# A streaming-encoder layer on one core: the first rows read in another order, the second half's rows two groups sooner

## The chip, the cores and the metric

The kernel runs on one core of a Trainium2 chip. A core has a tensor engine for matmuls (TensorE, PE in the profile), three engines for elementwise work (VectorE or DVE, ScalarE or ACT, GpSimd or POOL), and SyncE (SP), which here issues reads. All of them work through their own instructions in order and wait for each other by semaphores. Sixteen DMA engines move data between the main memory (HBM) and the two on-chip memories, SBUF and PSUM. The metric is the device time of one execution in microseconds; lower is better. Before the change it is 1509.12 us, the median of three runs (1508.5 to 1511.66).

## The reference

One layer of a hybrid encoder is computed for 2048 prompt tokens and 32 sample tokens, in float32. The model dimension is 1024.

```python
h = rmsnorm(x, ln_g)
(q, k, v, gate_a, b_gate, c_gate, u_in, gate_c, merge_a, merge_c) = jnp.split(h @ w_in, split_idx, axis=-1)
q = rope(rmsnorm(q.reshape(b, t, 8, 64), q_norm_g), pos)
k = rope(rmsnorm(k.reshape(b, t, 2, 64), k_norm_g), pos)
attn, new_k, new_v = attend(q, k, v, sink)         # chunks of 64, each sees itself and two before
u = c_gate * u_in
conv = causal convolution of u over 3 tokens       # with conv_past ahead of it
y_a = (attn * silu(gate_a)) @ w_attn_out
y_c = (b_gate * conv * silu(gate_c)) @ w_conv_out
r = x + (sigmoid(merge_a) * y_a + sigmoid(merge_c) * y_c) @ w_o
out = r + sigmoid(r @ w_ple_gate) * (p @ w_ple_proj)
```

`rmsnorm` divides by the root of the mean of squares over the 1024 columns of a token. The lines are cut from the reference; the one on the convolution is put in words.

## The kernel before

**Numbers and products.** Each float32 operand is split into a high part (a cast to `fp32r`, made on ACT) and a low part (the operand less its high part, made on DVE). A product is three matmuls: high by high, high by low, low by high. So each weight tile costs one cast and one subtraction ahead of its matmuls: `w<-wr` on ACT (L231 or L160), then on DVE (L232 or L160). For the projections a scheme of seven products instead of eight is used over two halves of the tokens and of the columns (a product is called p1 to p7). It needs sums of weight blocks (`make_sums`, L352 to L368: tiles `a7_0` to `a7_3` and `sc7` are those of group 7; `quad_sums`, L379 to L384: tiles `a11_58_2` and so on) and sums of rows of x. Groups of columns are numbered g = 0 to 20.

**Stages.** The opening, up to about 90 us, computes p @ w_ple_proj (`pp`, the pieces of the weight are `wppr` raw and `wpp0` to `wpp3` split) and the first mean of squares, and begins with the projection of the first half. Rows of x transposed (`b0_0` to `b0_7` for the first 512 tokens, `b1_0` to `b1_7` for the next) are read by `x_row`, squared (`sq`), added up on DVE, and summed over partitions on PE by eight matmuls with a column of ones (`pr`); `stats` makes the power on POOL, a diagonal (`dg`) on DVE, a transpose on PE (`rps`) and a copy on ACT (`rb`). Then the rows are normed. Up to about 440 us the first half of the tokens is projected, group by group. Then comes the second half, whose rows are read again from HBM (`refill`, tiles `xr`). From about 850 us on come the attention, its gates, and the out-projections.

**What sets the order.** In the opening and from the attention on, the order on every engine is written by a planner in the kernel's own Python code (`manual_schedule`): pieces of work are generators with a rank; each has a time at which it may go on, worked out from the assumed durations in `cost` (L104 to L118) and from what each engine and the DMA wire has been given so far. A lower rank goes first. The list `todo_loads` (L1086 to L1094) is the order of the opening's reads on SP; `stats` is started when eight squares are added, after a delay (L959). From L1254 on, the middle follows the order of the code, and the framework puts in the waits.

**The second half's rows.** A generator `X1 = second_half()` (L582) prepares the second half of the tokens while the first is projected. Its steps are: two means (`rms_rows`, each with ten reads `xt1_j_i_e` at L547, ten squares on ACT at L548, a small operation on DVE at L549, a power on POOL, `dg` at L530, `rps1_j` on PE at L532 and `rb` on ACT at L533), four combinations of rows that are stored to HBM (`xc`), and six steps for quarters (`quadrants`). One step is taken at the last product of a group: `prep = [at_step[0, g, 7] for g in range(7, G)]` (L1257), with G = 21. The scratch tiles (`tmp`) of all these come from one pool of 15 buffers, and SP reads into them in the order of the code, together with the weights.

**Attention.** `attention(e, when)` (L1402) works on 128 tokens. It reads `zq` and `zkv` (q, k and v of the tile) and `cs` (cosines and sines, 64 KB), waits for its time, transposes `zq` and `zkv` on PE (`pq`, `pkv`) and multiplies `cs` by the norm's gains on POOL. `next_loads` (L2008) issues further reads and starts weight splits as long as the planned backlog of ACT (`busy["S"]`) is short.

Of the kernel before, what the change touches and what calls it, by code (L numbers as in the profile page):

```python
# [9 lines left out]
AF = mybir.ActivationFunctionType  # L10
# [32 lines left out]
def tile_hybrid_stream_step(ctx: ExitStack, tc: tile.TileContext, x, xT, pT, wu, consts, rope, ckT, cv_dup,  # L43
# [60 lines left out]
    def cost(key, op, kw):  # L104
        if LATE["V"]:
            return cost_queue(key, op, kw)
        if op == "dma_start":
            return 0.9 if kw.get("accum_op") is not None else 0.57 if key == "G" else 0.42
        n = size(kw["out"])
        if key == "T":  # L110
            return max(0.109, 0.00044 * n + 0.0064)
        if key == "S":
            return 0.2 + 0.00082 * n + (0.13 if kw.get("accum_out") is not None else 0.0)
        if key == "G":
            return 2.03 if kw.get("op") == ALU.pow else 0.35 + 0.0021 * n
        if op == "tensor_reduce":
            return 0.08 + 0.0012 * size(kw["in_"])
        return 0.3 if n <= 16 else 0.13 + 0.0011 * n  # L118
# [51 lines left out]
    def free(tag, n=1):  # L170
        live[tag] -= n
        assert live[tag] >= 0, tag
# [758 lines left out]
    def wpp_piece(h):  # L931
        raw = quad(f"wppr{h}")
        eY.dma_start(out=raw, in_=wu[UPP + h // 2, :, 4 * (h % 2):4 * (h % 2) + 4, :])
        yield {"k": 2}
        wpp[h] = pair(f"wpp{h}")
        go(hilo0(wpp[h][0][:, :512], wpp[h][1][:, :512], raw.rearrange("p a b -> p (a b)"), ("wpp", h), lambda: free("wf")), None, None, -3 if h < 2 else -1)

# [5 lines left out]
    def x_row(j, k):  # L943
        v = B[k // 4, j, k % 4] = xrow(f"b{j}_{k}")
        eY.dma_start(out=v[:, :q0], in_=xT[k * P:(k + 1) * P, j * q0:(j + 1) * q0])
        yield {"k": 1, "@": "S"}
        sq = row(f"sq{j}_{k}")[:, :q0]
        eS.activation(out=sq, in_=v[:, :q0], func=AF.Square, scale=1.0 / 32.0)
        yield {}
# [8 lines left out]
        if ready[j] == 8:  # L958
            go(stats(j), now[0] + 1.8, None, j * 2 - 3)  # L959

# [82 lines left out]
    def sums0():  # L1043
# [10 lines left out]
        sums[0] = {7: sc, 5: a21, 6: a11, 3: a12, 4: a22}  # L1054
        for p, i in WS.items():
            eG.dma_start(out=wsum[0][:, i], in_=sums[0][p])
        for i in range(NP, NW):
# [12 lines left out]
    def split0(i):  # L1070
        while i > len(made):
# [16 lines left out]
                  ({}, (0, constants())), ({"wf": 1}, (-2, wpp_piece(2)))]  # L1088
    todo_loads += [({}, (-2, x_row(0, k))) for k in range(3, 8)] + [({"wf": 1}, (-1, wpp_piece(3)))]
    todo_loads += [({"wf": 1}, (0, raw0(i))) for i in range(2)] + [({"tmp": 1}, (0, p_row(1, k))) for k in range(2)]  # L1090
    todo_loads += [({"wf": 1}, (0, raw0(i))) for i in range(2, 5)]
# [164 lines left out]
    conv_at.update({(1, sets[-1], 3 + c % 2, "DE"[c // 2]): lambda c=c: conv_split(2, (c,)) for c in range(4)})  # L1256
    prep = [at_step[0, g, 7] for g in range(7, G)]  # L1257
    for i, todo in enumerate(steps):
# [140 lines left out]
    def attention(e, when):  # L1399
# [13 lines left out]
        cs = sm.tile([P, 2, 64], F32, tag="cs", name=f"cs{b}_{i}")  # L1413
        eY.dma_start(out=cs[:n], in_=rope[cols])
        landed_at = fin[0]
# [8 lines left out]
        for j in range(2):  # L1424
            eT.transpose(out=pkv[:n, j * P:(j + 1) * P], in_=zkv[:, j, :n], identity=ident)
        ab = sm.tile([P, 2, 2, 64], F32, tag="ab", name=f"ab{b}_{i}", bufs=1)
        eG.tensor_tensor(out=ab[:n], in0=cs[:n].unsqueeze(1).to_broadcast([n, 2, 2, 64]),
# [566 lines left out]
    def next_loads():  # L1994
# [36 lines left out]
        while n_split[0] < len(worder) and room["w"] > 0:  # L2031
# [11 lines left out]
            else:  # L2043
                if landed.get(i, 1e9) > now[0] or busy["S"] >= now[0] + (0.3 if i > used[0] + 2 else 1.5):
                    break
# [168 lines left out]
```

## Time and profile before

| what | value |
|---|---|
| median of three runs | 1509.12 us |
| the profiled execution | 1508.07 us |
| its span | 1506.0 us |
| mean granted clock of TensorE | 0.998 |
| data moved | 378.34 MB, 251 GB/s |
| longest single PE wait | 1.5 us |

The span is the time from the first to the last instruction in the profile. Busy times of the engines are shown further below, where they are used. A row of the timeline reads: start, duration, engine, line, operation, tiles written and read, shape, count, and in brackets the idle time before it and what ended it. A row of the windows reads: the stretch and its length, then the busy time and the number of instructions of PE, of the weight loads, of DVE, ACT and POOL, then the granted clock, the busy share of the DMA engines, and GB/s. The DMA engines by stretches of a fortieth of the span (37.65 us), in tenths, and the rate:

```profile
DMA  9469886898777987533578885687988959989959
GB/s 353 154 246 348 314 291 221 276 347 271 253 274 256 340 292 262 186 127 122 153 243 312 288 270 181 210 253 218 302 207 272 240 157 258 312 247 283 256 168 286
```

### The profile page before, as it was taken

The numbers are of one execution on the slowest core, as the hardware profiler recorded it, in microseconds if no ns is written. First come the engines' busy times: TensorE is split into PE (matmuls) and PEld (weight loads), VectorE is DVE, ScalarE is ACT, GpSimd is POOL, SyncE is SP. The second block draws the span as 40 slices with busy tenths as digits, with TensorE's granted clock in tenths as the row PEclk, the third lists the DMA queues.
The fourth block names the chain that finished last, engine by engine and source line by source line (L and its number), as shares of the span: only waits on it lengthen the run. The fifth ranks groups of instructions, "written<-read, shape, count | busy, mean of one in ns | idle before, by whom it ended". The sixth has DMA issues, their size and how long they took to land.

```text
span 1506.0 us, 28005 instructions
## 1 busy us (share of the span) xinstructions
PE 1489.3 (99%) x9553; PEld 1348.6 (90%) x9553; DVE 1210.7 (80%) x2308; ACT 803.7 (53%) x1910; POOL 399.0 (26%) x582
## 2 busy tenths in 40 slices
PE   9999999999999999999999999999999999999998
PEld 7878888888889999999999989998888788999998
DVE  7897887885579788799976878778899999676777
ACT  8453244344457655434455646687765686342453
POOL 2133332332211443433323311113232202211201
PEclk9999999999999999999999999999999999999999
DMA  9469886898777987533578885687988959989959
GB/s 353 154 246 348 314 291 221 276 347 271 253 274 256 340 292 262 186 127 122 153 243 312 288 270 181 210 253 218 302 207 272 240 157 258 312 247 283 256 168 286
DMA packets 206670, 378.34 MB, mean 251 GB/s; under 512 B 24896, under 2 KB 58496, under 8 KB 206528
## 3 DMA queue, kind: packets, MB, share of 16 engines
q1 hardware_dynamic: 160608, 258.30, 52.6%
q0 software_dynamic: 36272, 100.44, 22.2%
q10 hardware_dynamic: 9648, 17.83, 3.2%
q8 instruction: 75, 1.23, 0.3%
q14 instruction: 67, 0.55, 0.1%
HBM read 246.53 MB, written 130.04 MB: 250 GB/s over the span
## 4 chain that ended last, share of the span: by engine, by line
PE 91%; DMA 4%; DVE 2%; ACT 1%; issue 1%; POOL 0%; SPq 0%; DVEq 0%; ACTq 0%; POOLq 0%
PE b L160 21%; PE a L654 8%; PE a L651 7%; PE a L649 7%; PE yB L160 6%; PE yA L160 5%; PE la L787 5%; PE c L651 4%; PE c L649 4%; PE c L654 4%; PE lc L787 2%; PE pp L160 2%; PE O L160 2%; PE S L160 2%; PE PT L160 1%; PE lb L787 1%
## 5 line engine op out<-in xcount | busy, mean ns | idle before, releaser
L160 PE MATMUL b<-xb_h,w 128*128 128x264 f32 (+1 forms) x1344 | 310.7, 322 | 1.4 <-DVE at L160 1.4
L160 PEld LDWEIGHTS b<-xb_h,w 128*128 128x128 f32 x1344 | 222.7, 188 | 19.5 <-DVE at L160 1.9
L651 PE MATMUL a<-x_l,w 128*128 128x264 f32 (+1 forms) x744 | 228.2, 320 | 0.0
L649 PE MATMUL a<-x_h,w 128*128 128x264 f32 (+1 forms) x744 | 227.4, 320 | 0.2 <-ACT w L231 0.2
L160 PE MATMUL b<-xb_l,w 128*128 128x264 f32 (+1 forms) x672 | 216.6, 322 | 0.0
L654 PE MATMUL a<-x_h,w 128*128 128x264 f32 (+1 forms) x744 | 199.7, 321 | 0.9 <-DVE w L232 0.9
L231 ACT CAST w<-wr 128x512 fp32r<-128x512 f32 (+1 forms) x180 | 110.5, 619 | 96.2 <-PE c L654 34.9
L232 DVE TENSOR_TENSOR w<-wr,w 128x512 fp32r<-128x512 f32 (+1 forms) x180 | 133.2, 748 | 29.6 <-ACT w L231 28.0
L649 PEld LDWEIGHTS a<-x_h,w 128*128 128x128 f32 x744 | 139.9, 188 | 11.3 <-ACT w L231 0.4
L651 PEld LDWEIGHTS a<-x_l,w 128*128 128x128 f32 x744 | 140.0, 188 | 10.9
L654 PEld LDWEIGHTS a<-x_h,w 128*128 128x128 f32 x744 | 124.0, 188 | 11.9 <-DVE w L232 1.2
L160 PEld LDWEIGHTS b<-xb_l,w 128*128 128x128 f32 x672 | 126.4, 188 | 8.5
L160 ACT CAST w<-wr 128x512 fp32r<-128x512 f32 x120 | 73.6, 622 | 98.4 <-PE b L160 51.5
L787 PE MATMUL la<-x_h,w 128*128 128x264 f32 x516 | 111.3, 285 | 1.6 <-ACT w L231 1.6
L651 PE MATMUL c<-x_l,w 128*128 128x512 f32 (+1 forms) x336 | 110.9, 340 | 0.0
L649 PE MATMUL c<-x_h,w 128*128 128x512 f32 (+1 forms) x336 | 110.5, 339 | 0.0
L231 ACT CAST w<-a 128x512 fp32r<-128x512 f32 x82 | 49.8, 620 | 98.6 <-DVE a L364 33.2
L654 PE MATMUL c<-x_h,w 128*128 128x512 f32 (+1 forms) x336 | 100.1, 339 | 0.0
L160 DVE TENSOR_TENSOR w<-wr,w 128x512 fp32r<-128x512 f32 x120 | 83.6, 705 | 18.0 <-ACT w L160 17.7
L848 DVE SCALAR_TENSOR_TENSOR u<-u,c 128x264 f32<-128x264 f32 (+1 forms) x125 | 59.5, 507 | 42.8 <-ACT u L843 26.1
L160 PE MATMUL yB<-ycs_h,w 128*128 128x264 f32 (+1 forms) x384 | 91.0, 325 | 0.0
L160 PE MATMUL yA<-ac_h,w 128*128 128x264 f32 (+1 forms) x384 | 90.5, 323 | 0.0
(443 smaller groups left out, 3889.7 us busy)
## 6 DMA issues: line engine op xcount, KB each, us to landing
wr<-in_wu SPq DMA_DIRECT2D x161, 256.0 KB, 4.8
a<-in_wu SPq DMA_DIRECT2D x116, 256.0 KB, 5.3
wr<-ws SPq DMA_DIRECT2D x74, 256.0 KB, 4.0
w<-o SPq DMA_DIRECT2D x32, 512.0 KB, 4.7
ws<-a POOLq DMA_DIRECT2D x63, 256.0 KB, 4.3
w<-wa SPq DMA_DIRECT2D x16, 512.0 KB, 5.3
wr<-qs SPq DMA_DIRECT2D x32, 256.0 KB, 4.0
qs<-a POOLq DMA_DIRECT2D x24, 256.0 KB, 5.8
```

Of the source, the lines that this page charges most:

```text
L160: return f(**kw)
L231: nc.scalar.copy(out=hi, in_=src)
L232: nc.vector.tensor_tensor(out=lo, in0=src, in1=hi.bitcast(F32), op=sub)
L649: nc.tensor.matmul(out=ps[:, :cn], lhsT=w[:, 0, k], rhs=x[0][:, c0:c0 + cn], start=first and k == 0, stop=False, skip_group_check=True)
L651: nc.tensor.matmul(out=ps[:, :cn], lhsT=w[:, 0, k], rhs=x[1][:, c0:c0 + cn], start=False, stop=False, skip_group_check=True)
L654: nc.tensor.matmul(out=ps[:, :cn], lhsT=w[:, 1, k], rhs=x[0][:, c0:c0 + cn], start=False, stop=k == 3, skip_group_check=True)
L787: nc.tensor.matmul(out=ps[:, :m], lhsT=w[:, a, k], rhs=r[:, cols], start=q in "ABG" and j == 0 and e == 0, stop=j == 1 and e == 2, skip_gr ...
L848: nc.vector.scalar_tensor_tensor(out=t[:, c0:c0 + cn], in0=t[:, c0:c0 + cn], scalar=-1.0, in1=ps[:, :cn], op0=mul, op1=sub)
```

## The change

It computes the same. In the opening, the last piece of the `pp` weight (`wpp_piece(3)`) is read after row 5 instead of after row 7, and all four pieces have rank -3; the p rows of the second block are read ahead of the first two raw weights; the squares of rows 2 and 5 of the first mean are made on DVE; the second mean's statistics start without a delay and the first's with a shorter one; the stores of `sums0` become a piece of work of their own. The assumed duration of the power on POOL is 1.1 us in `cost`. In the middle, `prep` begins at group 5. In the attention, the first tile (`e == 0`) reads its `cs` after its transposes. In `next_loads`, the backlog of ACT may be longer for the weight that is used now.

```diff
--- before.py
+++ after.py
@@ -112,7 +112,7 @@
         if key == "S":
             return 0.2 + 0.00082 * n + (0.13 if kw.get("accum_out") is not None else 0.0)
         if key == "G":
-            return 2.03 if kw.get("op") == ALU.pow else 0.35 + 0.0021 * n
+            return 1.1 if kw.get("op") == ALU.pow else 0.35 + 0.0021 * n
         if op == "tensor_reduce":
             return 0.08 + 0.0012 * size(kw["in_"])
         return 0.3 if n <= 16 else 0.13 + 0.0011 * n
@@ -933,7 +933,7 @@
         eY.dma_start(out=raw, in_=wu[UPP + h // 2, :, 4 * (h % 2):4 * (h % 2) + 4, :])
         yield {"k": 2}
         wpp[h] = pair(f"wpp{h}")
-        go(hilo0(wpp[h][0][:, :512], wpp[h][1][:, :512], raw.rearrange("p a b -> p (a b)"), ("wpp", h), lambda: free("wf")), None, None, -3 if h < 2 else -1)
+        go(hilo0(wpp[h][0][:, :512], wpp[h][1][:, :512], raw.rearrange("p a b -> p (a b)"), ("wpp", h), lambda: free("wf")), None, None, -3)
 
     def constants():
         eY.dma_start(out=cst, in_=consts)
@@ -943,9 +943,13 @@
     def x_row(j, k):
         v = B[k // 4, j, k % 4] = xrow(f"b{j}_{k}")
         eY.dma_start(out=v[:, :q0], in_=xT[k * P:(k + 1) * P, j * q0:(j + 1) * q0])
-        yield {"k": 1, "@": "S"}
+        vector = j == 0 and k in (2, 5)
+        yield {"k": 1, "@": "V" if vector else "S"}
         sq = row(f"sq{j}_{k}")[:, :q0]
-        eS.activation(out=sq, in_=v[:, :q0], func=AF.Square, scale=1.0 / 32.0)
+        if vector:
+            eV.scalar_tensor_tensor(out=sq, in0=v[:, :q0], scalar=1.0 / 1024.0, in1=v[:, :q0], op0=mul, op1=mul)
+        else:
+            eS.activation(out=sq, in_=v[:, :q0], func=AF.Square, scale=1.0 / 32.0)
         yield {}
         if j not in acc0:
             acc0[j] = sq
@@ -956,7 +960,7 @@
             free("k")
         ready[j] = ready.get(j, 0) + 1
         if ready[j] == 8:
-            go(stats(j), now[0] + 1.8, None, j * 2 - 3)
+            go(stats(j), now[0] + 1.3 * (j == 0), None, j * 2 - 3)
 
 
     def stats(j):
@@ -1052,8 +1056,13 @@
             eV.tensor_tensor(out=o, in0=x, in1=y, op=add)
         yield {}
         sums[0] = {7: sc, 5: a21, 6: a11, 3: a12, 4: a22}
-        for p, i in WS.items():
-            eG.dma_start(out=wsum[0][:, i], in_=sums[0][p])
+        kept = dict(sums[0])
+
+        def keep():
+            for p, i in WS.items():
+                eG.dma_start(out=wsum[0][:, i], in_=kept[p])
+                yield {"@": "G"}
+        go(keep(), None, None, 2)
         for i in range(NP, NW):
             raw_of[i] = sums[0].pop(worder[i][3])
             go(split0(i), None, None, -0.5)
@@ -1086,8 +1095,9 @@
     todo_loads = [({"tmp": 1}, (-2, p_row(0, 0))), ({"tmp": 1}, (-2, p_row(0, 1))), ({"wf": 1}, (-3, wpp_piece(0))),
                   ({"wf": 1}, (-2, wpp_piece(1))), ({}, (-2, x_row(0, 0))), ({}, (-2, x_row(0, 1))), ({}, (-2, x_row(0, 2))),
                   ({}, (0, constants())), ({"wf": 1}, (-2, wpp_piece(2)))]
-    todo_loads += [({}, (-2, x_row(0, k))) for k in range(3, 8)] + [({"wf": 1}, (-1, wpp_piece(3)))]
-    todo_loads += [({"wf": 1}, (0, raw0(i))) for i in range(2)] + [({"tmp": 1}, (0, p_row(1, k))) for k in range(2)]
+    todo_loads += [({}, (-2, x_row(0, k))) for k in range(3, 6)] + [({"wf": 1}, (-2, wpp_piece(3)))]
+    todo_loads += [({}, (-2, x_row(0, k))) for k in (6, 7)] + [({"tmp": 1}, (-1, p_row(1, k))) for k in range(2)]
+    todo_loads += [({"wf": 1}, (0, raw0(i))) for i in range(2)]
     todo_loads += [({"wf": 1}, (0, raw0(i))) for i in range(2, 5)]
     todo_loads += [({}, (1, x_row(1, k))) for k in range(8)]
     todo_loads += [({"wf": 1}, (-1.5, raw0(i))) for i in range(5, 9)] + [({"wf": 4}, (-0.5, sums0()))]
@@ -1254,7 +1264,7 @@
     conv_at = {(1, G - 2, 1): lambda: conv_load(0), (1, G - 2, 6): lambda: (conv_split(0), conv_load(1)),
                (1, G - 1, 6): lambda: conv_split(1), (1, G - 2, 5): lambda: conv_load(2)}
     conv_at.update({(1, sets[-1], 3 + c % 2, "DE"[c // 2]): lambda c=c: conv_split(2, (c,)) for c in range(4)})
-    prep = [at_step[0, g, 7] for g in range(7, G)]
+    prep = [at_step[0, g, 7] for g in range(5, G)]
     for i, todo in enumerate(steps):
         if i < NS:
             continue
@@ -1411,7 +1421,8 @@
         zkv = tmp(f"zkv{b}_{i}", cols=256).rearrange("p (j c) -> p j c", j=2)
         eY.dma_start(out=zkv[:, :, :n], in_=z_q[:, 4:6, cols])
         cs = sm.tile([P, 2, 64], F32, tag="cs", name=f"cs{b}_{i}")
-        eY.dma_start(out=cs[:n], in_=rope[cols])
+        if e:
+            eY.dma_start(out=cs[:n], in_=rope[cols])
         landed_at = fin[0]
         while work[0] < when:
             yield {}
@@ -1423,6 +1434,8 @@
         pkv = bank(f"pkv{b}_{i}")
         for j in range(2):
             eT.transpose(out=pkv[:n, j * P:(j + 1) * P], in_=zkv[:, j, :n], identity=ident)
+        if e == 0:
+            eY.dma_start(out=cs[:n], in_=rope[cols])
         ab = sm.tile([P, 2, 2, 64], F32, tag="ab", name=f"ab{b}_{i}", bufs=1)
         eG.tensor_tensor(out=ab[:n], in0=cs[:n].unsqueeze(1).to_broadcast([n, 2, 2, 64]),
                         in1=qkg_sb[:n].unsqueeze(2).to_broadcast([n, 2, 2, 64]), op=mul)
@@ -2041,7 +2054,7 @@
                 eY.dma_start(out=w.bitcast(F32).rearrange("p a b c -> p a (b c)"), in_=src)
                 w_ready[i] = fin[0] + 0.5
             else:
-                if landed.get(i, 1e9) > now[0] or busy["S"] >= now[0] + (0.3 if i > used[0] + 2 else 1.5):
+                if landed.get(i, 1e9) > now[0] or busy["S"] >= now[0] + (0.3 if i > used[0] + 2 else 1.5 if i > used[0] + 1 else 5.0):
                     break
                 room["w"] -= 1
                 go(split_w(i))
```

What stands on PE in the opening, before. `p0_0` and `p0_1` are the two p rows, `wpp3` is the last piece, `pr0_0` is the first mean's sum over partitions:

```order
L160 MATMUL pp0_6_421<-p0_0_h_290,wpp3_h_379 128x512
L160 MATMUL pp0_6_421<-p0_0_l_291,wpp3_h_379 128x512
L160 MATMUL pp0_6_421<-p0_0_h_290,wpp3_l_380 128x512
L160 MATMUL pr0_0_431<-ones_72,sq0_0_302 128x1 x4
L160 MATMUL pp0_6_421<-p0_1_h_294,wpp3_h_379 128x512
L160 MATMUL pp0_6_421<-p0_1_l_295,wpp3_h_379 128x512
L160 MATMUL pp0_6_421<-p0_1_h_294,wpp3_l_380 128x512
L160 MATMUL pp0_7_446<-p0_0_h_290,wpp3_h_379 128x512
L160 MATMUL pp0_7_446<-p0_0_l_291,wpp3_h_379 128x512
L160 MATMUL pp0_7_446<-p0_0_h_290,wpp3_l_380 128x512
```

and now:

```order
L160 MATMUL pp0_6_421<-p0_0_h_290,wpp3_h_368 128x512
L160 MATMUL pp0_6_421<-p0_0_l_291,wpp3_h_368 128x512
L160 MATMUL pp0_6_421<-p0_0_h_290,wpp3_l_369 128x512
L160 MATMUL pp0_6_421<-p0_1_h_294,wpp3_h_368 128x512
L160 MATMUL pp0_6_421<-p0_1_l_295,wpp3_h_368 128x512
L160 MATMUL pp0_6_421<-p0_1_h_294,wpp3_l_369 128x512
L160 MATMUL pp0_7_435<-p0_0_h_290,wpp3_h_368 128x512
L160 MATMUL pp0_7_435<-p0_0_l_291,wpp3_h_368 128x512
L160 MATMUL pr0_0_442<-ones_72,sq0_0_302 128x1 x4
L160 MATMUL pp0_7_435<-p0_0_h_290,wpp3_l_369 128x512
```

The mean's products have moved five matmuls back, from within `pp0_6` to within `pp0_7`. On DVE in the opening, before (`sq0_k` is the square of row k; the sum is gathered in `sq0_0`):

```order
L160 TENSOR_TENSOR wpp1_l_299<-wppr1_252,wpp1_h_298 128x512
L160 TENSOR_TENSOR sq0_0_302<-sq0_0_302,sq0_1_307 128x512
L160 TENSOR_TENSOR sq0_0_302<-sq0_0_302,sq0_2_311 128x512
L160 TENSOR_TENSOR wpp2_l_318<-wppr2_260,wpp2_h_317 128x512
L160 TENSOR_TENSOR sq0_0_302<-sq0_0_302,sq0_3_325 128x512
L160 TENSOR_TENSOR sq0_0_302<-sq0_0_302,sq0_4_356 128x512
L160 TENSOR_TENSOR sq0_0_302<-sq0_0_302,sq0_5_363 128x512
L160 TENSOR_TENSOR sq0_0_302<-sq0_0_302,sq0_6_368 128x512
L160 TENSOR_SCALAR cst_69<-cst_69 128x64
L160 TENSOR_TENSOR sq0_0_302<-sq0_0_302,sq0_7_374 128x512
L160 TENSOR_TENSOR wpp3_l_380<-wppr3_272,wpp3_h_379 128x512
```

and now:

```order
L160 SCALAR_TENSOR_TENSOR sq0_2_311<-b0_2_258 128x512
L160 TENSOR_TENSOR sq0_0_302<-sq0_0_302,sq0_1_307 128x512
L160 TENSOR_TENSOR sq0_0_302<-sq0_0_302,sq0_2_311 128x512
L160 TENSOR_TENSOR wpp2_l_318<-wppr2_260,wpp2_h_317 128x512
L160 TENSOR_TENSOR sq0_0_302<-sq0_0_302,sq0_3_325 128x512
L160 SCALAR_TENSOR_TENSOR sq0_5_363<-b0_5_266 128x512
L160 TENSOR_TENSOR sq0_0_302<-sq0_0_302,sq0_4_356 128x512
L160 TENSOR_TENSOR sq0_0_302<-sq0_0_302,sq0_5_363 128x512
L160 TENSOR_TENSOR wpp3_l_369<-wppr3_268,wpp3_h_368 128x512
L160 TENSOR_TENSOR sq0_0_302<-sq0_0_302,sq0_6_377 128x512
L160 TENSOR_SCALAR cst_69<-cst_69 128x64
L160 TENSOR_TENSOR sq0_0_302<-sq0_0_302,sq0_7_385 128x512
```

Two squares have come in, and the low part of `wpp3` now stands ahead of the adds of rows 6 and 7; before, it stood behind all of them. On SP in the middle, from the raw weight 48 on, before:

```order
L352 DMA wr48_1747<-in_wu 128x512
L352 DMA a7_0_1817<-in_wu 128x512
L352 DMA a7_1_1819<-in_wu 128x512
L352 DMA a7_2_1821<-in_wu 128x512
L352 DMA a7_3_1823<-in_wu 128x512
L379 DMA a11_58_2_1800<-in_wu 128x512
L379 DMA a21_58_2_1802<-in_wu 128x512
L379 DMA a22_58_2_1804<-in_wu 128x512
L379 DMA a12_58_2_1806<-in_wu 128x512
L352 DMA wr54_1897<-in_wu 128x512
```

and now:

```order
L352 DMA wr48_1747<-in_wu 128x512
L547 DMA xt1_0_0_0_1769<-in_x 128x512
L547 DMA xt1_0_0_1_1772<-in_x 128x512
L547 DMA xt1_0_1_0_1775<-in_x 128x512
L547 DMA xt1_0_1_1_1778<-in_x 128x512
L352 DMA a7_0_1853<-in_wu 128x512
L547 DMA xt1_0_2_0_1781<-in_x 128x512
L547 DMA xt1_0_2_1_1784<-in_x 128x512
L352 DMA a7_1_1855<-in_wu 128x512
L547 DMA xt1_0_3_0_1787<-in_x 128x512
L352 DMA a7_2_1857<-in_wu 128x512
L352 DMA a7_3_1859<-in_wu 128x512
```

The ten reads of the second half's first mean (`xt1_0`) stand between `wr48` and the sums `58_2`; before, they came 18 reads later. On PE the end of their chain, `rps1_0`, stood between two products of group 8:

```order
L654 MATMUL a0_8_0_2030<-x0_5_1_h_1031,w62_2167 128x512
L649 MATMUL a0_8_0_2030<-x0_5_2_h_1035,w62_2167 128x512
L532 MATMUL rps1_0_0_2248<-cst_69,dg1_0_2251 128x128 x4
L532 MATMUL rps1_0_1_2249<-cst_69,dg1_0_2251 128x16
L651 MATMUL a0_8_0_2030<-x0_5_2_l_1036,w62_2167 128x512
L654 MATMUL a0_8_0_2030<-x0_5_2_h_1035,w62_2167 128x512
```

and now stands 127 rows earlier, between the last matmul of `w51` and the first of `w54`:

```order
L649 MATMUL a0_7_0_1919<-x0_6_3_h_989,w51_1887 128x512
L651 MATMUL a0_7_0_1919<-x0_6_3_l_990,w51_1887 128x512
L654 MATMUL a0_7_0_1919<-x0_6_3_h_989,w51_1887 128x512
L532 MATMUL rps1_0_0_1951<-cst_69,dg1_0_1954 128x128 x4
L532 MATMUL rps1_0_1_1952<-cst_69,dg1_0_1954 128x16
L649 MATMUL a0_8_0_2078<-x0_1_0_h_530,w54_1963 128x512
```

On SP at the start of the attention, before (`tb` are rows that pass through SBUF from the scratch tensor `z_t1` and back, `zq0_2` is the third tile's q):

```order
L160 DMA tb3_1_10494<-z_t1_1_109 128x528
L160 DMA z_t1_1_109<-tb0_1_10337 128x512
L160 DMA z_t1_1_109<-tb1_1_10389 128x512
L160 DMA zq0_2_10543<-z_q_77 128x4x128
L160 DMA zkv0_2_10545<-z_q_77 128x2x128
L160 DMA cs0_2_10547<-in_rope 128x128
```

and now:

```order
L160 DMA z_t1_1_109<-tb0_1_10335 128x512
L160 DMA tb3_1_10495<-z_t1_1_109 128x528
L160 DMA z_t1_1_109<-tb1_1_10394 128x512
L160 DMA tb0_2_10536<-z_t1_2_110 128x512
L160 DMA zq0_2_10549<-z_q_77 128x4x128
L160 DMA zkv0_2_10551<-z_q_77 128x2x128
```

`zq0_2` has one read more ahead of it, `tb0_2`.

## The prediction

> **What bounds the kernel now.** I began with the head of the page and its table of busy time, then took the list of waits of TensorE, since a kernel whose one engine never rests can only gain where that engine waits or runs slowly.
>
> ```profile
> span 1506.0 us, 28005 instructions
> PE 1489.3 (99%) x9553; PEld 1348.6 (90%) x9553; DVE 1210.7 (80%) x2308; ACT 803.7 (53%) x1910; POOL 399.0 (26%) x582
> ```
> ```profile
> PE la L787 <- ACT w L231: 1.6, 2, 1.1
> PE warm L1213 <- DVE ms L543: 1.5, 1, 1.5
> ...
> PE pp L160 <- ACT wpp_h L160: 1.4, 1, 1.4
> PE pq L160 <- DMA zq<-z_q: 1.2, 1, 1.2
> PE 1_0_461 L649 <- ACT x_h L160: 1.0, 1, 1.0
> PE lc L787 <- ACT w L231: 1.0, 3, 0.4
> ```
>
> The columns of the second fence are total, times and longest. TensorE (PE) is busy for 99% of the span, and the change takes no matmul away. So it can win waits, or time at a lower clock, and nothing else. The waits it could touch are 1.4 us at `pp` in the opening, 1.0 us at the first product that takes an x row of the second mean, 2.6 us at `la` and `lc` (the second half's refill) and 1.2 us at `pq` in the attention. All of them together are 6.2 us, 0.4% of the time. A measurement of this kernel tells about 0.2%, 3.0 us, from no change, and that is the bound which my three chances use.
>
> **The opening, where most of the gain lies.** The timeline of TensorE around the wait, and the windows behind it:
>
> ```profile
> 15.79 0.50 PE L160 MATMUL pp<-p_h,wpp_h 128*128 128x512 f32 x1 [1.38 <-ACT wpp_h L160]
> 16.13 0.40 PE L160 MATMUL pp<-p_l,wpp_h 128*128 128x512 f32 x1
> 16.52 0.50 PE L160 MATMUL pp<-p_h,wpp_l 128*128 128x512 f32 x1
> 16.86 0.95 PE L160 MATMUL pr<-ones,sq 128*128 128x1 f32 x8
> 17.66 0.50 PE L160 MATMUL pp<-p_h,wpp_h 128*128 128x512 f32 x1
> ```
> ```profile
> 14.00:18.00 4.00, 2.62 (x15) 1.69 (x14) 2.43 (x7) 4.00 (x9) 2.57 (x5) 1.00 1.04 388
> 18.00:20.00 2.00, 2.00 (x6) 1.61 (x5) 1.81 (x4) 1.70 (x4) 1.46 (x3) 0.50 1.05 405
> 20.00:21.00 1.00, 1.00 (x4) 0.71 (x4) 0.81 (x2) 0.16 (x1) 0.56 (x1) 0.50 1.05 420
> 21.00:22.00 1.00, 1.00 (x5) 0.81 (x4) 0.22 (x1) 0.41 (x1) 0.00 (x0) 0.80 1.04 416
> ```
> ```profile
> 210.13 0.40 PE L649 MATMUL a<-x_h,w 128*128 128x512 f32 x1
> 210.37 0.76 PE L532 MATMUL rps<-cst,dg 128*128 128x128 f32 x5
> ```
>
> A wide matmul in steady flow takes 0.24 us from start to start (210.13 to 210.37; more exactly 0.233, as 20 us hold some 86 of them). Three steps after the wait, 15.79 to 16.86, took 1.07 us instead of 0.70. After that the clock (the third column from the end) is 0.50 for 2 + 1 us and for 0.4 of the next one, so 3.4 us passed at half speed: 1.7 us lost. The wait, the slow steps and the half clock together cost 1.38 + 0.37 + 1.7 = 3.45 us.
>
> ```profile
> 11.94 2.32 ACT L160 ACTIVATE sq<-b 128x512 f32<-128x512 f32 x4
> 14.17 1.06 ACT L160 ACTIVATE pp<-pp 128x512 f32<-128x512 f32 x2
> 15.12 0.62 ACT L160 CAST wpp_h<-wppr 128x512 fp32r<-128x512 f32 x1
> ```
> ```profile
> 12.60 2.29 DVE L160 TENSOR_TENSOR sq<-sq,sq 128x512 f32<-128x512 f32 x3 [0.31 <-ACT sq L160]
> 14.98 0.69 DVE L160 TENSOR_TENSOR sq<-sq,sq 128x512 f32<-128x512 f32 x1
> ```
>
> The cast that PE waits for stands behind four squares and two evictions on ScalarE (ACT). In the change its raw piece is read two places earlier; at the 400 GB/s of the windows above a 256 KB read takes 0.66 us, so it lands 1.3 us sooner. Two squares have left ACT and the squares of rows 6 and 7 stand behind the cast. Its place is then near 13.0 to 13.6 us, before PE asks for it at 14.25. This wait goes.
>
> What is late next is VectorE (DVE). It gets two squares of about 0.7 us (an add of the same size takes 0.69; the square is not in the trace), and the low part `wpp3_l` now stands ahead of the adds of rows 6 and 7. PE takes `wpp3_l` with its third matmul, at 14.7 us; by the new row order it ends between 14.5 and 15.2, a wait of 0 to 0.5 us, and I take 0.3. Piece 2's low part, one square later than before, may cost the same again at 11.9 us; with it I take 0.5. The mean's products `pr` need the add of row 7. It ended at 15.67. Row 7 now lands one read, 0.66 us, later, which gives 16.3; if the two squares and `wpp3_l` all push it, 17.8. PE reaches `pr` after eight matmuls, at 16.1 plus the waits before. That is 0 to 1.7 us, and I take 0.4, near the lower end, because DVE had 0.31 us of idle time here and two squares of ACT no longer hold the adds up. The new waits come to 0.9 us, with ends of 0 and 2.2. Opening: 3.45 - 0.9 = **2.5 us gained**, between 1.2 and 3.4 if the clock holds.
>
> [...]
>
> **The second mean.** Its `rps` moves by one matmul in PE's order, and PE is 2.5 us sooner there, so both come sooner alike. The 1.0 us wait for `x_h` sits in this stretch:
>
> ```profile
> 60.00:100.00 40.00, 38.98 (x168) 31.16 (x167) 39.84 (x67) 22.83 (x42) 6.81 (x13) 1.00 0.48 168
> 150.00:170.00 20.00, 20.00 (x88) 16.10 (x87) 14.01 (x23) 6.21 (x11) 7.78 (x15) 1.00 0.94 320
> 170.00:190.00 20.00, 20.00 (x88) 16.14 (x87) 18.51 (x31) 4.89 (x10) 5.36 (x11) 1.00 0.86 314
> 190.00:210.00 20.00, 20.00 (x88) 16.15 (x87) 14.38 (x26) 12.72 (x32) 7.66 (x14) 1.00 0.92 339
> 470.00:490.00 20.00, 18.21 (x141) 17.31 (x140) 19.27 (x44) 15.53 (x37) 4.30 (x7) 1.00 0.76 250
> ```
>
> The third busy column is DVE: 39.84 of 40 us. An engine that full finishes when its work is done, not when its first operand comes; I count 0, with ends of 1.0 gained and 1.0 lost. `sums0`'s four stores now stand singly on POOL, busy 6.81 of 40 there: 0.
>
> **The second half's rows, two groups sooner.** This removes nothing. It moves ten reads (eight of 256 KB, two of 32 KB: 2.2 MB), their ten squares and the chain to `rps1_0`, and later the combinations.
>
> ```profile
> 149.46 0.50 SPq L352 DMA_DIRECT2D wr<-in_wu  x1
> 156.78 0.33 SPq L352 DMA_DIRECT2D a<-in_wu  x1
> ...
> 183.99 12.99 SPq L547 DMA_DIRECT2D xt<-in_x  x10
> ```
> ```profile
> 205.02 0.81 DVE L530 COPY dg<-rs 128x640 f32<-128x640 f32 x1
> ```
> ```profile
> 175.47 0.62 ACT L231 CAST w<-wr 128x512 fp32r<-128x512 f32 x1 [2.09 <-PE c L654]
> ```
>
> Before, the reads start at 183.99 and `dg` is done at 205.83: 21.8 us. Now they start behind `wr48`, at 150.0 at the soonest, and at 156.8 if the buffers that hold `a7_0` back hold them too; `dg` is ready at 171.8 to 178.6. `rps1_0` stands 127 rows earlier in PE's order: 210.37 - 127 x 0.233 = 180.8 us. It is in time by 2.2 to 9 us, if the transfers run as they did. But the windows 150 to 190 already have the DMA engines busy for 0.94 and 0.86, against 0.92 at the old place with the reads in it. The 2.2 MB take 6.4 us at 339 GB/s, and only 20 x 0.06 + 20 x 0.14 = 4.0 us are free. ACT has room (6.21 and 4.89 of 20 us). SP works in order, so the reads also hold up everything behind them: `a7`, the sums `58_2`, and `wr54`, whose cast ran at 175.47 and whose matmuls now follow `rps1_0` directly. Of the 13.0 us that ten reads took on SP, 6.8 (149.96 to 156.78) fall where SP waited anyway; 6.2 stay, against a lead of 180.8 - 175.5 - 1.3 (cast and low part) = 4.0 us. So the worst is 13.0 - 4.0 = 9.0 us of waiting, the middle 2.2. I take 0: half of the SP time before was itself waiting for stores, and by the order the first four reads take over buffers of older sums, stored by then. On the other side, the old place had no PE wait (20.00 of 20 in all three windows), so there is nothing to gain.
>
> At 470 to 490 PE loses 1.8 us to late weight casts. These rows come from stores that end well before; their reads wait for buffers, not for the earlier work. I count 0, with ends of 2.6 gained and 1.5 lost, for one cast moves behind two more rows on ACT.
>
> **The attention tile's sines.** The first `cs` read leaves its place, so four reads behind it go sooner; PE waited for none of them. In the burst after it, the order on SP puts `tb0_2` ahead of `zq0_2`.
>
> ```profile
> 881.77 0.37 SPq L160 DMA_DIRECT2D zq<-z_q  x1
> ...
> 883.75 0.35 SPq L160 DMA_DIRECT2D cs<-in_rope  x1
> 884.42 0.33 SPq L160 DMA_DIRECT2D tb<-z_t  x1
> ```
>
> A place costs 0.67 us (883.75 to 884.42), and PE waits for just this `zq` (1.2 us in the list): **0.7 us lost**, between 0 and 1.3. The looser limit in `next_loads` changes almost no row: 0. From there on PE's order is the same, and so is the tail.
>
> **Sum.** The profiled execution took 1508.07 us; 1508.1 - 2.5 + 0.7 = 1506.3. It lies 1.05 us below the median of the runs, 1509.12, so the forecast for a median is **1507.3**.
>
> **The rivals.**
> - The half clock stays, or falls in the next stretch because `wpp3_l`, `pr` and the one-column products leave gaps there: the opening wins 0.8, 1509.0. For it: nothing shows which part of the 2.2 us (wait and products) was decisive. Against it: idle time shrinks from 1.4 to 0.9, and the waits of 1.1 to 1.2 us elsewhere, `la` within 470 to 490 for one, left the clock at 1.00. [...] 15%.
> - The reads of the first mean delay `wr54` or `rps1_0`: slower. Place: PE at 180.8 us; it decides when SP is held for over 4.0 us beyond its old waits. Price 2.2 to 9.0 us, so 1509.5 to 1516.3, with its middle at 1512.5. For it: 0.94 of the DMA is taken. Against it: buffers bound SP there, not bandwidth alone. 17%.
> - The reads and the earlier chain also remove the waits at 83 us and in the refill (1.0 + 2.6): 1503.7. For it: everything of the second half is ready sooner. Against it: DVE is full at both places. 18%.
> - The moves come to nothing, as where a queue's first entry decides: this is the 0 of each part above, and within the forecast.
>
> **How the numbers follow.** The forecast, with its own spread of about 1.5 us to each side, has 50%. Below 1506.1 lie nearly all of the third rival and an eighth of the whole from the forecast's better end: faster 0.29. Above 1512.1 lies the greater part of the second rival and a little for what I have not seen: slower 0.14. The rest, 0.57, is no change. The range goes from the third rival, 1503.6, to about the middle of the second, 1511.9, and leaves some 2 in 10 out.
>
> **What would show it.** Right: no wait of `pp` on `wpp_h`, clock 1.00 from 18 to 21, no PE wait from 90 to 440, `pq` waiting 1.5 to 2. Wrong: a granted clock of 0.5 near 18, PE waiting for `dg` or `w` at 170 to 185, or `la` and `lc` gone from the list.

## The result, and the profile after

The changed kernel takes **1520.13 us** (median; 1519.46 to 1521.37) beside 1508.94 us for the kernel before: a ratio of 1.0071, with a 95% interval of 1.0054 to 1.0089. It is 11 us slower, above the predicted 1507.3 us and its range to 1511.9. Its profiled execution took 1519.46 us, with a span of 1517.6 us. The head of the page of the changed kernel:

```profile
span 1517.6 us, 28008 instructions
...
PE 1494.1 (98%) x9553; PEld 1350.3 (89%) x9553; DVE 1211.4 (80%) x2310; ACT 801.1 (53%) x1908; POOL 399.0 (26%) x582
```

The span grew by 11.6 us, but PE's busy time by only 4.8 with the same number of matmuls, so 6.8 us are new idle time, and the other 4.8 are the same matmuls at a lower pace. The list of TensorE's waits in the changed kernel (total, times, longest) names the idle time:

```profile
PE a L649 <- ACT u L843: 6.9, 2, 4.4
PE a L654 <- DVE w L232: 1.8, 2, 1.1
...
PE la L787 <- DVE s2n L803: 1.2, 1, 1.2
PE c L649 <- ACT x_h L160: 0.7, 1, 0.7
```

The first row is new: two waits of 6.9 us together for a copy `u` on ACT, which empties a PSUM bank that the next product `a` needs. The old waits for `wpp_h` and for `zq` are gone. To see where the time went, I take the windows of the changed kernel (the columns are those of the windows before):

```profile
14.00:18.00 4.00, 3.91 (x20) 2.80 (x19) 3.45 (x7) 3.95 (x9) 2.08 (x4) 1.00 1.05 395
18.00:20.00 2.00, 2.00 (x10) 1.61 (x9) 1.76 (x4) 2.00 (x5) 1.43 (x3) 1.00 1.06 401
...
150.00:170.00 20.00, 20.00 (x88) 16.16 (x87) 12.95 (x22) 10.36 (x25) 5.59 (x11) 1.00 1.04 396
...
260.00:280.00 20.00, 17.55 (x70) 13.75 (x69) 17.00 (x27) 6.03 (x11) 7.00 (x13) 0.91 0.82 277
...
300.00:320.00 20.00, 15.56 (x61) 12.26 (x60) 16.58 (x27) 5.11 (x10) 6.43 (x12) 0.91 0.77 263
...
268.00:271.00 3.00, 3.00 (x8) 2.31 (x7) 1.19 (x2) 1.10 (x2) 0.04 (x1) 0.50 0.97 290
...
313.00:315.00 2.00, 2.00 (x6) 1.54 (x6) 1.41 (x3) 0.51 (x1) 0.71 (x2) 0.50 0.96 345
```

The opening went as hoped: PE is busy for 3.91 of the 4 us from 14 to 18, and the granted clock is 1.00 behind it, where it was 0.50. The loss is between 260 and 320 us, where PE lacks 2.5 and 4.4 us. After each of the two waits the clock stands at 0.50 for some 3.4 us, which costs another 1.7 us each time. Together that is 6.9 + 3.4 = 10.3 us in two places. The kernel before had PE busy for 20.00 of 20 in every window there.

The second place in the timeline of the changed kernel, PE, then ACT, then DVE:

```profile
307.69 0.40 PE L654 MATMUL c<-x_h,w 128*128 128x512 f32 x1
312.53 0.80 PE L649 MATMUL a<-x_h,w 128*128 128x512 f32 x1 [4.44 <-ACT u L843]
...
310.85 1.14 ACT L231 CAST w<-a 128x512 fp32r<-128x512 f32 x2 [7.69 <-DVE a L364]
311.90 0.58 ACT L843 COPY u<-a 128x512 f32<-128x512 f32 x1
...
305.08 1.44 DVE L555 SCALAR_TENSOR_TENSOR b<-b,cst,rb 128x528 f32<-128x528 f32 x2
306.44 0.68 DVE L747 TENSOR_TENSOR cv<-s,cv 128x512 f32<-128x512 f32 x1
...
307.64 0.68 DVE L362 TENSOR_TENSOR sc<-a,a 128x512 f32<-128x512 f32 x1
308.24 0.70 DVE L559 TENSOR_TENSOR T<-b,b 128x528 f32<-128x528 f32 x1
308.86 0.68 DVE L363 TENSOR_TENSOR a<-a,a 128x512 f32<-128x512 f32 x1
309.46 0.70 DVE L560 TENSOR_TENSOR b<-b,b 128x528 f32<-128x528 f32 x1
310.08 0.68 DVE L364 TENSOR_TENSOR a<-a,a 128x512 f32<-128x512 f32 x1
```

Read it from the top. PE stands still from 308 until the copy `u` of 311.90. ACT is idle for 7.69 us before that: two casts `w<-a` stand ahead of the copy, and the first of them waits for `a L364`, the third addition of the weight sum of group 14. DVE makes this addition late, since from 303.13 us on it has no gap: it norms the rows of a combination (L555), adds the last tap of a convolution row (L726, among the rows left out), multiplies another by its gate (L747), and then alternates the additions of the weight sum (L362 to L364) with those of the combination (L559, L560). So a bank (the part of PSUM that holds one product here) waits for a copy, the copy for a cast in front of it, the cast for a sum, and the sum for the moved rows.

Why did the same crowd cost nothing before? There too a combination met the convolution rows of the same set, at 290 to 297 us. The timeline of ACT in the kernel before:

```profile
294.30 0.62 ACT L231 CAST w<-sc 128x512 fp32r<-128x512 f32 x1 [2.19 <-PE a L654]
297.09 0.62 ACT L231 CAST w<-a 128x512 fp32r<-128x512 f32 x1 [2.17 <-PE a L654]
297.62 0.58 ACT L843 COPY u<-a 128x512 f32<-128x512 f32 x1
301.60 0.62 ACT L231 CAST w<-a 128x512 fp32r<-128x512 f32 x1 [3.39 <-DVE a L364]
```

There too a cast waits for `a L364`, 3.39 us, and DVE alternates the same additions there (298.36 to 302.70); but the copy has been made ahead of that cast, and PE does not wait. ACT's order in the program shows the difference; numbers that grow in the order of the code stand at the names' ends, and `a_0_3026` and `a_0_3078` are the same tile, the sum of group 14. Before:

```
L231 CAST w_3043<-a_1_2843 128x512
L843 COPY u_12_2985<-a_12_0_2711 128x512
L231 CAST w_3065<-a_0_3026 128x512
```

and now:

```
L231 CAST w_3095<-a_1_2895 128x512
L231 CAST w_3117<-a_0_3078 128x512
L231 CAST w_3135<-a_3_2899 128x512
L843 COPY u_12_3037<-a_12_0_2763 128x512
```

In the code the copy (3037) comes ahead of the casts (3117) in both kernels. In the changed one the framework's own ordering issued the casts first.

### The profile page after: what moved, and what is told of

It is laid out like the page before. It is cut to its first block, busy times and chain, and to the rows that moved or that the text cites. A ratio compares the mean times of both kernels' runs of the same rounds, so it can differ in the third digit from the quotient of the medians.

```text
span 1517.6 us, 28008 instructions
## 1 busy us (share of the span) xinstructions
PE 1494.1 (98%) x9553; PEld 1350.3 (89%) x9553; DVE 1211.4 (80%) x2310; ACT 801.1 (53%) x1908; POOL 399.0 (26%) x582
## 4 chain that ended last, share of the span: by engine, by line
PE 71%; DVE 3%; DMA 3%; issue 1%; ACT 1%; POOL 0%; SPq 0%; ACTq 0%; DVEq 0%; POOLq 0%
PE b L160 21%; PE yB L160 6%; PE yA L160 6%; PE a L649 5%; PE a L654 5%; PE a L651 5%; PE la L787 4%; PE O L160 2%; PE c L654 2%; PE c L651 2%; PE c L649 2%; PE lc L787 2%; PE S L160 2%; PE pp L160 2%; PE PT L160 1%
```

## The experiments

Each kernel below is the changed one with the edit shown, unless the text says otherwise. The first question was which part of the change costs the time.

**The changed kernel with `prep` as before**

```diff
-    prep = [at_step[0, g, 7] for g in range(5, G)]
+    prep = [at_step[0, g, 7] for g in range(7, G)]
```

> The changed kernel with the second half's preparation back at group 7; all other edits stay. Theory A (the loss is in the middle: the combinations of rows, two groups sooner, stand on VectorE ahead of a weight sum in groups in which the convolution stands there too) and theory B (the loss is in the middle: the early reads hold up the DMA and SP) both expect 1505 to 1507 us, 2 to 4 us under the kernel before: no PE wait over 0.5 us from 90 to 440. Theory C (another edit costs the time: opening, attention, next_loads) expects 1515 us or more.

It took 1504.74 us, a ratio to the kernel before of 0.997 (0.9959 to 0.998), and beats both kernels. It is a little below the range expected. The list of TensorE's waits has no row from 90 to 440 us. The windows of this kernel:

```profile
260.00:280.00 20.00, 20.00 (x88) 16.17 (x88) 16.31 (x25) 6.72 (x12) 7.00 (x14) 1.00 0.92 316
...
300.00:320.00 20.00, 20.00 (x88) 16.15 (x87) 17.51 (x29) 8.41 (x15) 6.97 (x13) 1.00 0.93 317
```

**The kernel before, with only `prep` begun at group 5**

```diff
-    prep = [at_step[0, g, 7] for g in range(7, G)]
+    prep = [at_step[0, g, 7] for g in range(5, G)]
```

> The kernel before with nothing changed but the preparation, which begins at group 5. Theories A and B expect 1520 to 1524 us (the loss of the change without what the opening gained), with PE waiting for ACT u near 266 and 310. Theory C expects 1507 to 1511.

1519.93 us, ratio 1.0074 (1.0059 to 1.009). The list of TensorE's waits in this kernel has the same row on top:

```profile
PE a L649 <- ACT u L843: 6.6, 2, 4.0
```

One number, 7 or 5, is the whole loss. With 7, all the other parts of the change together gain some 4.6 us (1504.74 against 1509.32 in the same comparison). With 5 they gain nothing that shows (1520.13 against 1519.93): in the traces the changed kernel is 2.5 us ahead of this one at the 151st matmul, and at the 2500th, at 536.6 us, both are level. Part of that is the clock. This kernel's shorter wait, 2.59 us, brought no half clock (1.00 from 260 to 280 us); the 2.45 us of the changed kernel did. TensorE in this kernel:

```profile
268.33 0.50 PE L649 MATMUL a<-x_h,w 128*128 128x512 f32 x1 [2.59 <-ACT u L843]
```

**The means early, the combinations as late as before**

```diff
-    prep = [at_step[0, g, 7] for g in range(5, G)]
+    prep = [at_step[0, g, 7] for g in (5, 6, 7, 8, *range(11, G))]
```

> The changed kernel, the two means at groups 5 to 8 as in the change, but the combinations and quarters from group 11 on as before. Theory A expects 1506 to 1509 us: the waits at 264 and 308 go, those near 178 and 215 (0.4 and 1.2 us) may stay. Theory B (reads) expects 1515 to 1520.

1506.99 us, ratio 0.9985 (0.9975 to 0.9994). In this kernel PE waits at 178 us for `dg`, at 215 us for a low part from DVE, and for a cast:

```profile
PE a L654 <- DVE w L232: 1.1, 1, 1.1
PE a L649 <- ACT w L231: 0.4, 1, 0.4
PE rps L532 <- DVE dg L530: 0.3, 1, 0.3
```

The early means cost 1506.99 - 1504.74 = 2.3 us, and these three rows are 1.8 us of it. The early combinations cost the other 1520.13 - 1506.99 = 13.1 us (11.4 by the spans, 1517.6 against 1506.2).

**The combinations at groups without convolution rows**

```diff
-    prep = [at_step[0, g, 7] for g in range(5, G)]
+    prep = [at_step[0, g, 7] for g in (5, 6, 7, 8, 9, 11, *range(13, G))]
```

> The changed kernel, the two means at groups 5 to 8, the four combinations at groups 9, 11, 13 and 14, so that none follows the convolution's rows in its group, quarters from group 15 on. Theory A expects 1506 to 1510 us with no PE wait over 1 us at 250 to 330, although two combinations come two groups and one group sooner. If being sooner costs in itself (theory A'), one or two waits of 2 to 5 us stay: 1511 to 1518. Theory B expects 1515 to 1520.

1508.12 us, ratio 0.9993 (0.9983 to 1.0002). Both long waits are gone, though the first combination is still as early as in the change. So an early place brings no long wait by itself, as the combinations of groups 9 and 11 show; what counts is which DVE work meets there.

**The combinations from the fifth product of a group on**

```diff
-    prep = [at_step[0, g, 7] for g in range(5, G)]
+    prep = [at_step[0, g, 7] for g in range(5, 9)] + [at_step[0, g, 4] for g in range(9, G)]
```

> The changed kernel, means at groups 5 to 8 as in the change, but the combinations and quarters of groups 9 to 20 are issued after product 4 of their group instead of after product 7, some 11 us later. The convolution's rows of sets 2 and 3 then share the stretch between two weight sums on VectorE with the first and the third combination, not with the second and the fourth. Theory A1 (what counts is how much work VectorE has between two weight sums) expects the two PE waits on ACT u to stay, 2 to 5 us each, at about 245 and 285: 1513 to 1521 us. Theory A2 (what counts is the place right behind product 7) expects them gone: 1506 to 1509 us.

1516.31 us, ratio 1.0045 (1.0031 to 1.0059). That is within the first theory's range, but the waits are not where it put them: they stand at 298 and 302 us, not at 245 and 285, and have a neighbour's name. In this kernel's list:

```profile
PE a L649 <- ACT s L843: 2.9, 1, 2.9
PE c L654 <- DVE w L232: 1.3, 1, 1.3
```

Moving the rows within the group wins 3.8 us and does not remove the loss. Another bank pays.

**Less work on DVE: the combinations' norms left out**

```diff
-                    norm(b[s, j][:, :q], kk, rb[j], q)
```

> The changed kernel without the four normings of rows ahead of each combination of the second half (16 VectorE operations of 0.76 us left out; the second half's rows are then not normed, the outputs of the second half differ). Theory A1 expects the PE waits at 264 and 308 to shrink by the 2.7 us that VectorE saves in each: 0 to 0.3 and 1 to 2.2 us, no half clock at 268; 1508 to 1513 us. A theory in which the stores or reads of these rows are the cause (POOL, SP, DMA) expects both waits as they were and 1518 to 1521.

1506.61 us, ratio 0.9989 (0.9979 to 0.9999). Both waits are gone, and the time is below the range expected. Sixteen operations of 0.77 us, less than 13 us of DVE time, give back 13.5 us of the kernel's. The reads and stores of these rows are still there, so they are not the cause.

**Less work on DVE: two taps of the convolution rows left out, in sets 2 and 3 of the first half**

```diff
-                    for e in (1, 2):
+                    for e in (1, 2) if h or n < 2 else ():
```

> The changed kernel without two of the three taps of the convolution in the first half's sets 2 and 3 (8 VectorE operations of 0.75 us left out, 4 in each set; part of the convolution's output differs). If the convolution's rows are the other half of the crowd (theory A1), the waits at 264 and 308 shrink by 2.6 us each, as without the normings: 1508 to 1513 us. If only the combinations matter, nothing moves: 1518 to 1521.

1511.21 us, ratio 1.0012 (1.0002 to 1.0022). The wait at 264 us is gone, and that at 308 us (here at 302) is 1.2 us long. So the convolution rows, which the change does not touch, are as much a part of the crowd as the moved rows. DVE's backlog is a condition of the loss. How the backlog reaches PE was open: through the order on ACT, or by the sum itself being late.

**The eviction ahead of the casts on ACT** (an eviction empties a bank; the lines that note the last one in `evicted`, and the branch for all other weights, are left out)

```diff
+            if evicted[0] is not None and i in (84, 91, 98):
+                with tc.issue_after(evicted[0]):
+                    split(w[:, 0, :n], w[:, 1, :n], raw_of.pop(i)[:, :n])
```

> The changed kernel with one thing fixed: for three weight parts (the first of groups 12, 13 and 14) the cast on ScalarE may only be issued after the last eviction copy of u that stands ahead of it in the program. On ScalarE u40_10 then stands ahead of w84, and u40_12 ahead of w98, as in the kernel before; u40_11 stays ahead of w91, where it stood. The rows, the sums and VectorE's work are the same and stay at the same groups. Theory (the wait is a chain: TensorE for a bank, the bank for the copy, the copy behind a cast, the cast for a sum, the sum behind the rows): with the copy out of that queue the waits at 264 and 308 us are gone or below 0.5 us each, no half clock follows them, and the time is 1506 to 1509.5 us, near the kernels whose rows were moved away. Rival (VectorE is simply late with the sum, and the products that need the sum wait whatever ScalarE's order): the waits come back under another name, TensorE waiting for the weight part itself, at about 2 and 4 us, and the time stays at 1516 to 1521 us.

1516.23 us, ratio 1.0045 (1.0027 to 1.0062). The time is at the lower edge of what the rival gives, but the waits are not the rival's. The wait at 264 us is gone, and PE is busy for 19.62 of 20 us from 260 to 280. At 307 us a wait of 2.9 us came back under another name. TensorE's waits in this kernel have on top:

```profile
PE c L654 <- DVE u L854: 3.3, 2, 2.9
PE la L792 <- DVE s2n L808: 2.4, 1, 2.4
```

The second row lies outside the crowd, in the refill at 499 us, where the changed kernel waits 1.2 us; a half clock of 3.4 us follows it here. Some 2.9 us of this execution's 1517.74 us (2.4 - 1.2 + 1.7) come from there, and the four executions lie between 1514.02 and 1519.08, so the median says less than the trace. L854 is the subtraction `u<-u,c` on DVE. The timeline of DVE in this kernel:

```profile
307.37 0.68 DVE L364 TENSOR_TENSOR a<-a,a 128x512 f32<-128x512 f32 x1
307.97 0.70 DVE L566 SCALAR_TENSOR_TENSOR T<-b,b 128x528 f32<-128x528 f32 x1
308.59 0.68 DVE L365 TENSOR_TENSOR a<-a,a 128x512 f32<-128x512 f32 x1
309.19 0.70 DVE L567 SCALAR_TENSOR_TENSOR T<-T,b 128x528 f32<-128x528 f32 x1
309.81 0.68 DVE L854 SCALAR_TENSOR_TENSOR u<-u,c 128x512 f32<-128x512 f32 x1
```

This subtraction empties the bank of the `c` products. The last of these started at 304.48 and `u` was copied at 301.90, yet it ran at 309.81, behind the same sum (L364, L365) and the same combination (L566, L567). ACT's order was the link at the first place. At the second, DVE's own order is another.

**The eviction ahead of the sum on DVE too** (edit on top of the last one)

```diff
-        nc.vector.tensor_tensor(out=sc, in0=a11, in1=a21, op=add)
+        with tc.issue_after(evicted[1]) if g in (12, 13, 14) else nullcontext():
+            nc.vector.tensor_tensor(out=sc, in0=a11, in1=a21, op=add)
```

> The last kernel with the same thing done on VectorE too: for groups 12, 13 and 14 the first addition of the weight sum may only be issued after the last eviction (the subtraction u<-u,c, which frees a bank of the c products) that stands ahead of it in the program. In VectorE's order that eviction of groups 10, 11 and 12 then stands ahead of the sum and no longer behind it. All work stays, at the same groups. Theory (VectorE's backlog of rows and sums is the cause, and the queue order says which bank pays; TensorE waits only where an eviction stands behind the sum): the wait of 3 us at 307 us falls below 0.8, no half clock follows, and the time is 1508 to 1513 us, since the small waits at 215, 238, 267 and 292 us (together some 3.3 us) stay. Rival (work that VectorE cannot do in time has to hold TensorE somewhere): the sum itself is late, TensorE waits 2 us or more for a weight part after 305 us, and the time stays at 1514 to 1519 us.

1511.09 us, ratio 1.0011 (1.0002 to 1.0021). In this kernel no wait of PE is longer than 1.1 us from 90 to 440 us; the list of that stretch begins:

```profile
PE a L662 <- DVE w L233: 2.2, 2, 1.1
PE b L657 <- ACT w L232: 1.9, 2, 1.0
```

and its windows have the clock at 1.00:

```profile
300.00:320.00 20.00, 18.40 (x78) 14.25 (x78) 18.55 (x30) 7.98 (x14) 7.05 (x13) 1.00 0.72 251
```

The same instructions at the same groups, with two evictions issued ahead of late sums, take 9.0 us less than the changed kernel (by the medians; by the spans, 1517.6 and 1509.9, it is 7.7). The rival holds in part: waits of about 1 us for weight parts remain, and the kernel stays 4.1 us behind the one with early means and late combinations (1506.99).

**The sines read ahead again** (the first of these kernels, `prep` from group 7, with the attention as before)

```diff
-        if e:
-            eY.dma_start(out=cs[:n], in_=rope[cols])
+        eY.dma_start(out=cs[:n], in_=rope[cols])
...
-        if e == 0:
-            eY.dma_start(out=cs[:n], in_=rope[cols])
```

> The kernel with the preparation back at group 7 (1504.7 us), and the first attention tile's sines read ahead of its transposes again. Theory D (the sines' place freed SP and so brought the third tile's q in time) expects a PE wait of pq on zq of about 1 us again and 0.5 to 1.5 us more than 1504.7. Theory E (the q wait depends on when the burst falls, not on the sines) expects no change beyond 0.3 us.

1506.27 us, ratio 0.9985 (0.9976 to 0.9994), so 1.5 us more than with the sines behind; the two intervals overlap a little, and the ratios alone would leave it open. The traces point the same way. In this kernel's timeline the third `pq` waits, and a half clock of 3.4 us follows (886.6 to 890.1 us); but this execution took 1508.12 us, 1.85 above the kernel's median, so it shows more than the usual loss:

```profile
886.69 1.09 PE L160 MATMUL pq<-cst,zq 128*128 128x128 f32 x4 [2.28 <-DMA zq<-z_q]
...
880.26 0.37 SPq L160 DMA_DIRECT2D zq<-z_q  x1
```

and with the sines behind it does not:

```profile
885.44 0.63 PE L160 MATMUL pq<-cst,zq 128*128 128x128 f32 x4
...
879.71 0.37 SPq L160 DMA_DIRECT2D zq<-z_q  x1
```

## Why the prediction was wrong

**What bounds the kernel: right, but read one way only.** With PE busy for 99%, I listed the waits that the change could win. The same figure says that any lateness which uses up PE's slack costs its full length, and I did not go through the moved work with that question.

**The opening: the number right, one term by luck.** 2.5 us were forecast. The 151st matmul of PE, in the timeline of before and of after:

```profile
40.42 0.39 PE L160 MATMUL pp<-p_h,wpp_l 128*128 128x512 f32 x1
```

```profile
37.75 0.39 PE L160 MATMUL pp<-p_h,wpp_l 128*128 128x512 f32 x1
```

It starts 2.67 us sooner. The signs named for the opening came, no wait for `wpp_h` and a clock of 1.00 from 18 us on, and with them small new waits at the third matmul of `wpp3` and at `pr`, in the changed kernel's timeline:

```profile
14.70 0.39 PE L160 MATMUL pp<-p_l,wpp_h 128*128 128x512 f32 x1
15.19 0.50 PE L160 MATMUL pp<-p_h,wpp_l 128*128 128x512 f32 x1
...
16.46 0.39 PE L160 MATMUL pp<-p_l,wpp_h 128*128 128x512 f32 x1
16.83 1.02 PE L160 MATMUL pr<-ones,sq 128*128 128x1 f32 x8
```

The steps of 0.49 and 0.37 us stand for 0.23 each, so 0.26 and 0.14 us were lost against the 0.3 and 0.4 taken for them. That the half clock, 1.7 of the 3.45 us, would go with the wait was an estimate from one trace. It did go, but it did not bind. In the run with the old opening and the early `prep` it did not come in the profiled execution, and the 151st matmul started at 40.23 all the same: PE came sooner to the first x row and waited there for its low part. TensorE in that run:

```profile
28.71 0.50 PE L160 MATMUL 1_0_461<-x_l,w 128*128 128x512 f32 x1 [0.81 <-DVE x_l L160]
```

In the kernel before this matmul started at 29.00 and in the changed kernel at 27.72, both times without a wait. So in the old opening the x row is ready at about the time at which PE came after its half clock, and the gain needs the row a microsecond sooner. The prediction does not work that out; which of the edits did that was not tried. The other executions of the kernel before agree: in 25 of the 68 listed with the experiments (an outlier of 6337 us is left out) the mean clock is given as 1.0, which has no room for 3.4 us at half speed (they alone would take it to 0.9989), and the median of these, 1509.12 us, is that of the rest, 1509.10.

**The second half's rows: wrong, and this is the step that failed.** "It moves ten reads (...), their ten squares and the chain to `rps1_0`, and later the combinations." The reads, the squares and the chain got a price; the last four words got none. I took 0 from the side of SP and its buffers, found "nothing to gain" since "the old place had no PE wait", and asked of the new place only whether SP, the DMA engines and ACT had room. The combinations are work of DVE, and they moved from groups 11 to 14 to groups 9 to 12, where the convolution rows of sets 2 and 3 come due. The combinations' move cost 13.1 us, and the means' 2.3 us.

The slower rival had the wrong place. It expected `wr54` or `rps1_0` to come late at 180 us for 2.2 to 9 us. The reads did go through (396 GB/s from 150 to 170 us, a DMA share of 1.04), and `rps1_0` waited 0.3 us. The early means do cost what the rival's lower end says, but mostly at 215 us, for DVE's low part. Why DVE is late there was not tried further.

**What turned a backlog into 10 us.** The load of DVE over a long stretch does not tell it: over 260 to 320 us DVE is busy for 47.97 us in the changed kernel and 52.24 us in the one with `prep` from 7, which loses nothing (PE stood still for part of the first, so less work came due). Two things are needed, and runs show both. One is the crowd of a few operations at one place: without the norms the waits go, without the taps they shrink to 1.2 us. The other is the order on each engine's queue (the subtraction `u` ran at 309.81 behind the sum, though its product's last matmul had started at 304.48): with one eviction moved ahead one wait goes, with two moved ahead no wait is longer than 1.1 us, at the same work; and in the kernel before the same additions met with the copy already made. The order is not all of it, since with both evictions ahead the kernel stays 4.1 us behind the one with late combinations. That the ordering put the casts ahead of the copy because of its own estimates of when the sum would be ready is likely, but only argued.

**The attention's sines: the sign was wrong, as far as the pair shows.** I counted one place on SP that `zq0_2` loses, 0.7 us lost. In the pair above its read is issued 0.55 us sooner with the sines behind (879.71 against 880.26), and `pq` starts 1.25 us sooner, at 885.44. What failed here is that one read's place in the list was taken for its time. What else the planner moved ahead of it was not separated.

**The refill and the second mean: right.** `la` and `lc` wait for 3.0 us from 440 to 520 us in the changed kernel (1.2 + 0.7 + 0.6 + 0.5 with the rows below those shown), 2.6 before; the wait for `x_h` at 83 us, 1.0 us, became two, 0.7 and 0.5. Two slips of the working move nothing: the third rival's time stands as 1503.7 and as 1503.6, and the middle of 1509.5 and 1516.3 is 1512.9, not 1512.5.

## What to carry to other kernels

When work is moved, list its instructions on every engine, and lay them beside what already comes due at the new place; here the load of DVE over 60 us said little (47.97 us with the loss, 52.24 without), and a few operations in front of one eviction decided. Follow each PSUM bank that the next products need back through the queue in which its eviction stands: if a cast or a sum that may be late can be issued ahead of that eviction, the eviction waits with it, as the copy `u` of 311.90 us did behind the casts that could start only at 310.85. Here evictions first took 9.0 us of the loss away. The better version is simpler still: the change without its one number for `prep`, 1504.74 us.

## What the runs showed of the hardware

- The granted clock fell to 0.50 for 3.4 us after idle stretches of PE of 2.45 us (at 264 us in the changed kernel), 2.9 and 2.4 us (at 307 and 499 us, with the eviction first on ACT only), 2.9 us (at 302 us, with the combinations later in the group) and 2.28 us (at 884 us, with the sines read ahead), and after the longest, 4.44 us, for as long. It stayed at 1.00 after one of 2.59 us (at 266 us, with only `prep` begun at 5) and where the stretches were about 1.1 us long. In the kernel before it stood at 0.50 from 18.0 to 21.4 us, behind a stretch of 1.38 us that ended at 15.79 and eight one-column products at 16.86. So of the six stretches of 2.28 to 2.9 us five were followed by the half clock and one was not: the length alone did not decide here. With the 1.7 us that such a half clock took, the wait of 2.45 us cost some 4.1 us.
